# Fillers that shift the transposed activations against multiples of 256 bytes in SBUF, with the weight buffers left where they are

## The chip, the cores and the metric

The kernel runs on one NeuronCore of a Trainium2 chip. The metric is the device time of one execution in microseconds. Three runs of the kernel before took 1163.83, 1164.23 and 1167.16 us; the median is 1164.23 us.

## The reference, cut to what matters

Two transformer blocks run one after the other on 256 tokens of width 1024 in float32. The products that carry most of the arithmetic are these:

```
# first block, layer 0 (attention) and layer 1 (pooling), each followed by a gated feed-forward of width 2816
k, v, q = hx @ w_qkv ...            # with modulation of x by c @ w_mod
x = layer_norm(ALPHA * x + g1 * y)
x = layer_norm(ALPHA * x + g2 * (silu(h @ w_in_g) * (h @ w_in_u)) @ w_out)
# second block
u = rms_norm(x) @ w_in              # sixteen 512-wide slices and one of width 16 (g_lr)
y = sigmoid(gate_a) * y_a + sigmoid(gate_b) * y_b
x = x + y @ w_out
x = x + square(relu(rms_norm(x) @ w_up)) @ w_down      # width 4096
x = x + sigmoid(rms_norm(x) @ w_ple_gate) * (p @ w_ple)
```

Every product has 256 rows of tokens, so every weight is used for two groups of 128 tokens (called t = 0 and t = 1 in the code).

## The kernel before, in words

**Weights.** All weights come in blocks of 128 partitions x 1024 float32 (4096 bytes per partition) in one planned order. `Stream.dma` brings a block into one of eight `raw` buffers. `Stream.split` turns it into two float32r tiles: `hi` (ScalarE copy, L287) and `lo` = raw - hi (VectorE subtraction, L293), eight buffers each. The 80 blocks of modulation weights are reduced on VectorE instead (L271).

**Products.** The operand that TensorE keeps in its array (the stationary operand) is a piece of 128 tokens x 128 features of the transposed activations; the weights stream past it (the moving operand), 512 columns at a time. Each float32 product is made of three float32r matmuls: activation-high x weight-high, activation-high x weight-low, activation-low x weight-high. `mmN` (L378 to L380) does this for a product that is summed over eight pieces into one `mm` tile; `mmK` (L392, L394) and `mmK_tail` (L405 to L407) do it for one row block of weights into the two halves of a `big` tile. Each matmul has a weight load (LDWEIGHTS, shown as PEld) of its own. In the profile `mm<-hi,xTh` is a matmul with moving operand `hi` and stationary operand `xTh`. A few products are done in plain float32, with one instruction in the code and two matmuls in the trace; `keep` (L218) is a filler of that kind, on the tile `crow`.

**Transposed activations.** `xTh` and `xTl` hold the high and low part of the 256 transposed tokens (8 pieces of 256 columns, 8192 bytes per partition each). They are filled by `tr_half`: four transposes on TensorE into a `tr` tile, then a ScalarE copy (L427 or L739) and a VectorE subtraction (L428 or L741). In the feed-forward parts the hidden values are transposed by `tr` (L984) and `trm` (L1608) into `hh0`, `hl0` (t = 0) and `hh1`, `hl1` (t = 1), two buffers each, filled by L427 and L428. Other stationary tiles are `hch`, `hcl` (shown as `xa`, `s`) in the first projections and `obT`, `qkd` in two products of the second block.

**Order.** The order of the instructions on each engine is the order of the program text; `Stream.pump` puts the splitting of further blocks behind each use of a block.

**Where tiles lie.** A tile's address within a partition follows from the pools: pools are stacked in the order in which they are opened, the tiles of a pool follow one another in the order in which their tags first appear, and each starts at a multiple of 32 bytes. In the compiled kernel before, `xTh` starts at byte 18432, `xTl` at 26624, `cst` (identity matrix and tables) at 34816, `crow` at 36160, the eight `raw` at 43008, the eight `hi` at 75776, the eight `lo` at 108544, `xa` at 141312 and `s` at 149504. In the last feed-forward `hh0` starts at 175616, `hl0` at 179712, `hh1` at 183808, `hl1` at 187904 and the output tile `sg` at 192000. The filler tile `pad` ahead of `raw` and the wide `half` tile ahead of `xTh` hold nothing that is used (of `half`, 8 columns are). Of the tiles named, all but `crow` start at a multiple of 256 bytes; `crow` and the `gtmp` tiles of the second block start 64 bytes past one. The low-rank gate product `g_lr` (L1425) uses pieces of 16 columns (64 bytes) of a weight block as the stationary operand, which lie 0, 64, 128 and 192 bytes past multiples of 256 in turn.

Of the kernel before, what the change touches and what calls it, by code (L numbers as in the profile page):

```python
# [10 lines left out]
F32R = mybir.dt.float32r  # L11
# [7 lines left out]
P = 128  # L19
# [154 lines left out]
def body(ctx: ExitStack, tc: tile.TileContext, wst, prm, cst, cst2, poolp, xT_d, cT_d, x_d, head, lam_d,  # L174
# [23 lines left out]
    cp = Pool("cp")  # L198
    ctx.callback(cp.close)
    rg = Pool("rg")  # L200
# [7 lines left out]
    def mmt():  # L208
        return pp.t([P, 512], "mm")

    def trt():
        return pp.t([P, 512], "tr")
# [10 lines left out]
    prm_s = cp.t([P, PRM_W], "prm")  # L223
    mc = [cp.t([P, 48], f"mc{l}") for l in range(2)]
    half_e = cp.t([P, 184], "half")[:, :8]
    xTh = cp.t([P, KD, T], "xTh", F32R)
    xTl = cp.t([P, KD, T], "xTl", F32R)
    cst_s = cp.t([P, CST_W], "cst")
    crow = cp.t([P, D], "crow")
    raw0 = rg.t([P, 368], "pad")  # L230
    G.memset(half_e, -0.5)

    def prmc(n):
# [6 lines left out]
    def is32(key):  # L240
        return key[0] in F32B or (key[0] == "WO" and key[1] // 4 in WOF) or (
            key[0] == "G" and key[2] == 0 and key[1] in GF)
# [116 lines left out]
    def mmN(ps, lh, keys, width=512, off=0, cols=None, mid={}):  # L359
        per = BW // width  # L360
        cols = cols or width
        n = len(keys)
        for i, key in enumerate(keys):
            w32 = st.get32(key) if is32(key) else None
            hi, lo = st.get(key) if w32 is None else (None, None)
            for j in range(per):
                k = i * per + j
                if k in mid:
                    mid[k]()
                if w32 is not None:  # L370
                    TE.matmul(ps, lh(k), w32[:, j * width + off:j * width + off + cols], start=k == 0,
                              stop=i == n - 1 and j == per - 1)
                    continue
                sl = slice(j * width + off, j * width + off + cols)
                h, l = lh(k)
                s = k == 0
                e = i == n - 1 and j == per - 1
                TE.matmul(ps, h, hi[:, sl], start=s, stop=False)  # L378
                TE.matmul(ps, h, lo[:, sl], start=False, stop=False)  # L379
                TE.matmul(ps, l, hi[:, sl], start=False, stop=e)  # L380
# [15 lines left out]
    def mmK_tail(halves, lhs, keys, first=False):  # L396
        for f in range(2):
            sl = slice(f * 512, (f + 1) * 512)
            for i, (lh, key) in enumerate(zip(lhs, keys)):
                if is32(key):  # L400
                    TE.matmul(halves[f], lh, st.get32(key)[:, sl], start=first and i == 0, stop=i == len(keys) - 1)
                    continue
                h, l = lh
                hi, lo = st.get(key)
                TE.matmul(halves[f], h, hi[:, sl], start=first and i == 0, stop=False)  # L405
                TE.matmul(halves[f], h, lo[:, sl], start=False, stop=False)  # L406
                TE.matmul(halves[f], l, hi[:, sl], start=False, stop=i == len(keys) - 1)  # L407

    def halves(ps):
        return [ps[:, 0:512], ps[:, 512:1024]]  # L410

    def xlh(t):
        return lambda k: (xTh[:, k, t * P:(t + 1) * P], xTl[:, k, t * P:(t + 1) * P])

    def mkey(k, n):
        return [k + (i,) for i in range(n)]
# [8 lines left out]
    def split_evac(ps, dh, dl, scale=None):  # L425
        if scale is None:
            A.activation(dh, ps, AF.Copy)  # L427
            V.tensor_tensor(dl, ps, dh.bitcast(F32), op=OP.subtract)  # L428
        else:
            A.activation(dh, ps, AF.Copy, scale=scale)  # L430
            V.scalar_tensor_tensor(dl, ps, scale, dh.bitcast(F32), op0=OP.mult, op1=OP.subtract)
# [372 lines left out]
    for i in range(n_it + 5):  # L804
# [25 lines left out]
        if 3 <= i <= n_it + 2:  # L830
            t, h = items[i - 3]
# [3 lines left out]
        if i >= 5 and items[i - 5][1] % 4 == 3:  # L835
            t, f = items[i - 5][0], items[i - 5][1] // 4
# [108 lines left out]
    def ffn(l, fp, x1_ready, after0, mid1, after1, mid):  # L945
        J = len(FFN_CHUNKS)
        ops_ = None
        hT = {}
        hs = {}

        def gu(j, t, which, ps, mid={}):
            c0, w = FFN_CHUNKS[j]
            n = D * w // (P * BW)
            lh = xlh(t)
            if is32((which, l, j)):
                lh = lambda k: xf[t, k // 4][:, k % 4]
            mmN(ps[:, :w], lh, mkey((which, l, j), n), width=w, mid=mid)

        def do_g(j, t):
            ps = mmt()  # L960
            gu(j, t, "G", ps)
            w = FFN_CHUNKS[j][1]
            h = fp.t([P, 512], f"h{t}", bufs=2)
            A.activation(h[:, :w], ps[:, :w], AF.Silu)  # L964
            hs[j, t] = h

        def do_u(j, t, mid={}):
            ps = mmt()
            gu(j, t, "U", ps, mid)
            w = FFN_CHUNKS[j][1]  # L970
            h = hs[j, t]
            V.tensor_tensor(h[:, :w], h[:, :w], ps[:, :w], op=OP.mult)  # L972

        def fin(j, which):
            c0, w = FFN_CHUNKS[j]
            st.done(*mkey((which, l, j), D * w // (P * BW)))

        def tr(j, t):
            w = FFN_CHUNKS[j][1]
            n = w // P  # L980
            h = hs.pop((j, t))
            ps = trt()
            for i in range(n):
                TE.transpose(ps[:, i * P:(i + 1) * P], h[:, i * P:(i + 1) * P], ident)  # L984
            hh = fp.t([P, 4, P], f"hh{t}", F32R, bufs=2)
            hl = fp.t([P, 4, P], f"hl{t}", F32R, bufs=2)
            pv = ps.rearrange("p (k t) -> p k t", t=P)[:, :n]
            split_evac(pv, hh[:, :n], hl[:, :n])
            hT[j, t] = (hh, hl)

        def o(j, t, done):
            n = FFN_CHUNKS[j][1] // P
            hh, hl = hT.pop((j, t))
            if j == J - 1:
                keys = [("O", l, j, i) for i in range(n)]
                mmK_tail(halves(ops_[t]), [(hh[:, i], hl[:, i]) for i in range(n)], keys)
                if done:
                    st.done(*keys[:HN[l]])
                    st.hold = True
                    st.done(*keys[HN[l]:])  # L1000
                return
            for i in range(n):
                mmK(halves(ops_[t]), (hh[:, i], hl[:, i]), ("O", l, j, i), j == 0 and i == 0, False)
                if done:
                    st.done(("O", l, j, i))

        for j in range(J):
            if j == 0:
                do_g(0, 0)
                do_u(0, 0, {XR[l]: x1_ready})  # L1010
                if XR[l] == 8:
                    x1_ready()
                do_g(0, 1)
                fin(0, "G")
                do_u(0, 1)
                fin(0, "U")
                ops_ = [big(), big()]
            else:
                do_g(j, 0)
                if j == 1:  # L1020
                    tr(0, 1)
                do_g(j, 1)
                fin(j, "G")
                do_u(j, 0)
                do_u(j, 1)
                fin(j, "U")
            if j in mid:
                mid[j]()
            if j < J - 1:
                if j > 0:  # L1030
                    o(j - 1, 0, False)
                tr(j, 0)
                if j > 0:
                    o(j - 1, 1, True)
                    tr(j, 1)
            else:
                tr(j, 0)
                o(j - 1, 0, False)
                tr(j, 1)
                o(j, 0, False)  # L1040
                if l == 0:
                    for b in range(2):
                        st.prescale(("PW", b))
                after0(ops_[0])
                if l == 0:
                    st.hold = True
                o(j - 1, 1, True)
                mid1()
                o(j, 1, True)
                after1(ops_[1])  # L1050
                if l == 1:
                    st.hold = False
                    st.pump()

    fp = Pool("fp")
# [474 lines left out]
    for i, (c, t) in enumerate(seq):  # L1530
        f = int(c[2])
# [55 lines left out]
    fp = Pool("fp3")  # L1587
# [16 lines left out]
    def trm(j, t):  # L1604
        h = hs.pop((j, t))
        ps = trt()
        for i in range(4):
            TE.transpose(ps[:, i * P:(i + 1) * P], h[:, i * P:(i + 1) * P], ident)  # L1608
        hh = fp.t([P, 4, P], f"hh{t}", F32R, bufs=2)
        hl = fp.t([P, 4, P], f"hl{t}", F32R, bufs=2)  # L1610
        split_evac(ps.rearrange("p (k t) -> p k t", t=P), hh, hl)
        hT[j, t] = (hh, hl)

# [161 lines left out]
```

## Time and profile before

| | |
|---|---|
| median of three runs | 1164.23 us |
| profiled execution: its own time | 1166.95 us |
| its span, first to last instruction | 1165.2 us |
| TensorE matmul busy | 1120.5 us, 96% |
| TensorE weight load busy | 884.0 us, 76% |
| VectorE, ScalarE busy | 761.2 us (65%), 560.0 us (48%) |
| mean granted TensorE clock | 0.991 |

A group row of the profile gives line, engine, operation, tile names, shape and count, then busy time and mean duration of one, then idle time before them and what ended it. The duration of a matmul reaches from its first read to a modelled end; successive matmuls overlap, so the distance from start to start is what one matmul costs in a chain. Such distances are read from the timeline.

### The profile page before, as it was taken

To read this page: it belongs to the slowest core of one execution; us is meant where nothing else is said; L and a number is where in the kernel's file an instruction comes from. 1 tells how busy PE (TensorE), PEld (TensorE's weight loads), DVE (VectorE), ACT (ScalarE), POOL (GpSimd) and SP (SyncE) were. 2 spreads that over 40 slices of the span, in tenths; PEclk is the share of its full clock that TensorE was granted. 3 is DMA by queue.
4 is the path that set the end of the run, shared out by engine and by line. 5 is a ranking of instruction groups with operands and counts; after the bars stand their busy time and mean duration, and the time that the engine had idled before them with its cause. 6 is when DMAs were issued, how large, how long until landed. Compare 5 with 4: busy or idle time off the path is not lost. (4 is left out here: it accounts for less than half of the span.)

```text
span 1165.2 us, 14166 instructions
## 1 busy us (share of the span) xinstructions
PE 1120.5 (96%) x5186; PEld 884.0 (76%) x5186; DVE 761.2 (65%) x1114; ACT 560.0 (48%) x913; POOL 22.7 (2%) x35
## 2 busy tenths in 40 slices
PE   7989988899999999999999999999999999999998
PEld 4578665578888876888887687877778877888887
DVE  7988858668886675577446765454545875455555
ACT  3552456454344426534444755457235464444453
POOL 0000000000000000000000110000000000000000
PEclk9999899999999999999999999998999999999999
DMA  9887813669897806568463755452444645454520
GB/s 348 310 275 253 288 57 136 214 224 344 300 392 261 294 20 215 196 225 298 169 226 128 234 194 184 146 167 91 145 145 137 215 154 187 176 201 164 212 93 37
DMA packets 65922, 234.62 MB, mean 201 GB/s; under 512 B 7323, under 2 KB 8347, under 8 KB 65852
## 3 DMA queue, kind: packets, MB, share of 16 engines
q1 hardware_dynamic: 63936, 227.84, 55.2%
q10 hardware_dynamic: 1916, 5.87, 1.5%
q8 instruction: 41, 0.67, 0.2%
q14 instruction: 29, 0.24, 0.1%
HBM read 232.63 MB, written 1.05 MB: 201 GB/s over the span
## 5 line engine op out<-in xcount | busy, mean ns | idle before, releaser
L293 DVE TENSOR_TENSOR lo<-raw,hi 128x1024 fp32r<-128x1024 f32 x316 | 374.6, 1220 | 126.2 <-ACT hi L287 121.8
L287 ACT ACTIVATE hi<-raw 128x1024 fp32r<-128x1024 f32 x316 | 323.1, 1057 | 106.6 <-PE mm L380 56.8
L378 PE MATMUL mm<-hi,xTh 128*128 128x512 f32 (+1 forms) x872 | 339.7, 390 | 7.3 <-ACT xTh L427 4.0
L380 PE MATMUL mm<-hi,xTl 128*128 128x512 f32 (+1 forms) x872 | 334.0, 383 | 2.0 <-DVE xTl L428 1.6
L379 PE MATMUL mm<-lo,xTh 128*128 128x512 f32 (+1 forms) x872 | 333.4, 382 | 1.9 <-DVE lo L293 1.9
L378 PEld LDWEIGHTS mm<-hi,xTh 128*128 128x128 f32 x872 | 165.4, 190 | 45.0 <-ACT xTh L427 5.9
L380 PEld LDWEIGHTS mm<-hi,xTl 128*128 128x128 f32 x872 | 165.1, 189 | 36.1 <-DVE xTl L428 3.3
L379 PEld LDWEIGHTS mm<-lo,xTh 128*128 128x128 f32 x872 | 165.6, 190 | 33.5 <-DVE lo L293 3.4
L271 DVE SCALAR_TENSOR_TENSOR raw<-raw,crow 128x1024 f32<-128x1024 f32 x80 | 96.6, 1218 | 0.0
L392 PE MATMUL big<-hi,hh 128*128 128x512 f32 x256 | 80.6, 396 | 0.0
L392 PE MATMUL big<-lo,hh 128*128 128x512 f32 x256 | 79.2, 391 | 0.0
L394 PE MATMUL big<-hi,hl 128*128 128x512 f32 x256 | 79.0, 390 | 0.0
L427 ACT ACTIVATE hh<-tr 128x512 fp32r<-128x512 f32 (+1 forms) x40 | 23.0, 575 | 84.8 <-PE tr L1608 42.6
L428 DVE TENSOR_TENSOR hl<-tr,hh 128x512 fp32r<-128x512 f32 (+1 forms) x40 | 26.3, 660 | 48.8 <-ACT hh L427 48.0
L394 PEld LDWEIGHTS big<-hi,hl 128*128 128x128 f32 x256 | 48.1, 188 | 10.4
L392 PEld LDWEIGHTS big<-lo,hh 128*128 128x128 f32 x256 | 48.0, 188 | 10.3
L964 ACT ACTIVATE h<-mm 128x512 f32<-128x512 f32 (+1 forms) x24 | 13.4, 563 | 84.1 <-PE mm L380 83.9
L392 PEld LDWEIGHTS big<-hi,hh 128*128 128x128 f32 x256 | 46.7, 188 | 8.6
L422 POOL TENSOR_TENSOR st<-st,half 128x4 f32<-128x4 f32 (+1 forms) x28 | 21.8, 778 | 1045.1 <-DVE st L420 1032.0
L1601 DVE TENSOR_TENSOR h<-h 128x512 f32<-128x512 f32 x16 | 11.0, 688 | 33.6 <-ACT h L1600 33.5
L1600 ACT ACTIVATE h<-mm 128x512 f32<-128x512 f32 x16 | 9.6, 599 | 38.0 <-PE mm L380 38.0
L972 DVE TENSOR_TENSOR h<-h,mm 128x512 f32<-128x512 f32 (+1 forms) x24 | 15.3, 640 | 18.7 <-PE mm L380 18.6
(316 smaller groups left out, 1254.1 us busy)
## 6 DMA issues: line engine op xcount, KB each, us to landing
raw<-in_dram SPq DMA_DIRECT2D x426, 512.0 KB, 5.1
row<-in_dram ACTq DMA_DIRECT2D x8, 512.0 KB, 7.3
tok<-in_dram SPq DMA_DIRECT2D x8, 256.0 KB, 6.9
xa<-in_dram SPq DMA_DIRECT2D x2, 512.0 KB, 5.1
out_dram<-sg SPq DMA_DIRECT2D x3, 256.0 KB, 2.0
pmat<-in_dram ACTq DMA_DIRECT2D x1, 544.0 KB, 12.4
crow<-in_dram ACTq DMA_DIRECT2D x1, 512.0 KB, 4.8
out_dram<-sg SPq DMA_DIRECT2D x2, 128.0 KB, 1.7
```

What stands on the lines that cost most here:

```text
L271: V.scalar_tensor_tensor(raw, raw, 1.0, crow, op0=OP.mult, op1=OP.mult, accum_out=mc[l][:, nb:nb + 1])
L287: A.activation(hi, raw, AF.Copy)
L293: V.tensor_tensor(lo, raw, hi.bitcast(F32), op=OP.subtract)
L378: TE.matmul(ps, h, hi[:, sl], start=s, stop=False)
L379: TE.matmul(ps, h, lo[:, sl], start=False, stop=False)
L380: TE.matmul(ps, l, hi[:, sl], start=False, stop=e)
L392: TE.matmul(halves[f], h, w[:, f * 512:(f + 1) * 512], start=first and b == 0, stop=False)
L394: TE.matmul(halves[f], l, hi[:, f * 512:(f + 1) * 512], start=False, stop=last)
L422: G.tensor_tensor(r, v, half_e[:, :w], op=OP.pow)
L427: A.activation(dh, ps, AF.Copy)
L428: V.tensor_tensor(dl, ps, dh.bitcast(F32), op=OP.subtract)
L972: V.tensor_tensor(h[:, :w], h[:, :w], ps[:, :w], op=OP.mult)
```

## The change

Two filler tiles of 64 bytes are put ahead of `xTh` and between `xTh` and `xTl`, and the filler ahead of the weight buffers is made 128 bytes shorter. The `hh` tiles get 32 and the `hl` tiles 64 unused bytes at their end, so that each later buffer of the pool moves on by as much. The access patterns, the instructions and their order stay.

```diff
     half_e = cp.t([P, 184], "half")[:, :8]
+    pad1 = cp.t([P, 16], "pad1")
     xTh = cp.t([P, KD, T], "xTh", F32R)
+    pad2 = cp.t([P, 16], "pad2")
     xTl = cp.t([P, KD, T], "xTl", F32R)
     cst_s = cp.t([P, CST_W], "cst")
     crow = cp.t([P, D], "crow")
-    raw0 = rg.t([P, 368], "pad")
+    raw0 = rg.t([P, 336], "pad")
...
# in tr (feed-forward of the first block) and in trm (second block)
-            hh = fp.t([P, 4, P], f"hh{t}", F32R, bufs=2)
-            hl = fp.t([P, 4, P], f"hl{t}", F32R, bufs=2)
+            hh = fp.t([P, 4 * P + 8], f"hh{t}", F32R, bufs=2)[:, :4 * P].rearrange("p (k t) -> p k t", t=P)
+            hl = fp.t([P, 4 * P + 16], f"hl{t}", F32R, bufs=2)[:, :4 * P].rearrange("p (k t) -> p k t", t=P)
```

## Rows read from the trace of the kernel before

**Rows 1.** The page: span, busy time of the engines, granted clock in 40 slices.
```profile
span 1165.2 us, 14166 instructions
...
PE 1120.5 (96%) x5186; PEld 884.0 (76%) x5186; DVE 761.2 (65%) x1114; ACT 560.0 (48%) x913; POOL 22.7 (2%) x35
...
PEclk9999899999999999999999999998999999999999
```

**Rows 2.** Groups by line: matmuls and weight loads on the transposed activations.
```profile
L378 PE MATMUL mm<-hi,xTh 128*128 128x512 f32 (+1 forms) x872 | 339.7, 390 | 7.3 <-ACT xTh L427 4.0 <-ACT aT L686 1.5 <-ACT mv L1378 1.2
L380 PE MATMUL mm<-hi,xTl 128*128 128x512 f32 (+1 forms) x872 | 334.0, 383 | 2.0 <-DVE xTl L428 1.6 <-DVE xTl L741 0.4
L379 PE MATMUL mm<-lo,xTh 128*128 128x512 f32 (+1 forms) x872 | 333.4, 382 | 1.9 <-DVE lo L293 1.9
...
L379 PEld LDWEIGHTS mm<-lo,xTh 128*128 128x128 f32 x872 | 165.6, 190 | 33.5 <-DVE lo L293 3.4 <-issue 0.2
...
L392 PE MATMUL big<-hi,hh 128*128 128x512 f32 x256 | 80.6, 396 | 0.0
...
L394 PE MATMUL big<-hi,hl 128*128 128x512 f32 x256 | 79.0, 390 | 0.0
...
L405 PE MATMUL big<-hi,hh 128*128 128x512 f32 x48 | 19.1, 398 | 0.0
...
L392 PE MATMUL big<-hi,xTh 128*128 128x512 f32 x48 | 16.2, 420 | 3.6 <-ACT tok L616 3.6
```

**Rows 3.** Timeline (start, duration, engine, line): matmuls and a load in mid-chain.
```profile
900.42 0.39 PE L378 MATMUL mm<-hi,xTh 128*128 128x512 f32 x1
900.42 0.19 PEld L379 LDWEIGHTS mm<-lo,xTh 128*128 128x128 f32 x1
...
903.82 0.39 PE L378 MATMUL mm<-hi,xTh 128*128 128x512 f32 x1
```

**Rows 4.** Timeline: the first matmuls behind a group of transposes, last feed-forward.
```profile
1005.44 0.63 PE L392 MATMUL big<-lo,hh 128*128 128x512 f32 x2
1005.91 0.62 PE L394 MATMUL big<-hi,hl 128*128 128x512 f32 x2
1006.37 0.62 PE L392 MATMUL big<-hi,hh 128*128 128x512 f32 x2
```

**Rows 5.** Timeline of L1425: stationary pieces of 16 columns, third and last row block.
```profile
781.30 0.28 PE L1425 MATMUL mm<-xTh,hi 128*16 128x256 f32 x1
...
783.23 0.28 PE L1425 MATMUL mm<-xTl,hi 128*16 128x256 f32 x1
```

**Rows 6.** Timeline: feed-forward matmuls of 256 columns, stationary pieces of 128 columns.
```profile
323.27 0.28 PE L378 MATMUL mm<-hi,xTh 128*128 128x256 f32 x1
...
324.59 0.28 PE L380 MATMUL mm<-hi,xTl 128*128 128x256 f32 x1
```

**Rows 7.** Timeline and group row of the filler matmuls on crow.
```profile
426.96 2.31 PE L218 MATMUL tr<-crow 128*128 128x512 f32 x5
...
L218 PE MATMUL tr<-crow 128*128 128x512 f32 x10 | 4.5, 592 | 0.0
```

**Rows 8.** Groups by line: VectorE and ScalarE on tiles at different addresses.
```profile
L427 ACT ACTIVATE hh<-tr 128x512 fp32r<-128x512 f32 (+1 forms) x40 | 23.0, 575 | 84.8 <-PE tr L1608 42.6 <-PE tr L984 42.1
...
L428 DVE TENSOR_TENSOR hl<-tr,hh 128x512 fp32r<-128x512 f32 (+1 forms) x40 | 26.3, 660 | 48.8 <-ACT hh L427 48.0
...
L525 DVE SCALAR_TENSOR_TENSOR junkb<-raw,ropeb 128x1024 bf16<-128x1024 f32 x16 | 19.4, 1219 | 0.0
L525 DVE SCALAR_TENSOR_TENSOR junkb<-raw,crow 128x1024 bf16<-128x1024 f32 x16 | 19.0, 1220 | 1.2 <-DMA raw<-in_dram 1.1
...
L1600 ACT ACTIVATE h<-mm 128x512 f32<-128x512 f32 x16 | 9.6, 599 | 38.0 <-PE mm L380 38.0
...
L1552 ACT ACTIVATE gtmp<-mm 128x512 f32<-128x512 f32 x4 | 2.4, 600 | 9.1 <-PE mm L380 9.0
```

**Rows 9.** DMA issues: the last stores of the result, with KB and time to landing.
```profile
out_dram<-sg SPq DMA_DIRECT2D x2, 128.0 KB, 1.7
```

More of the change, by code (lines that the diff above doesn't have):

```diff
@@ L1608, in trm @@
             TE.transpose(ps[:, i * P:(i + 1) * P], h[:, i * P:(i + 1) * P], ident)
-        hh = fp.t([P, 4, P], f"hh{t}", F32R, bufs=2)
-        hl = fp.t([P, 4, P], f"hl{t}", F32R, bufs=2)
+        hh = fp.t([P, 4 * P + 8], f"hh{t}", F32R, bufs=2)[:, :4 * P].rearrange("p (k t) -> p k t", t=P)
+        hl = fp.t([P, 4 * P + 16], f"hl{t}", F32R, bufs=2)[:, :4 * P].rearrange("p (k t) -> p k t", t=P)
         split_evac(ps.rearrange("p (k t) -> p k t", t=P), hh, hl)
```

## The prediction

> **What bounds the kernel now.** I read the page first. TensorE is busy for 96% of the span, at a granted clock of nine tenths or more, the level of 2.4 GHz, in all but two of 40 slices; the other engines have a third or more of the span to spare [rows 1]. So the span is in the main the number of matmuls times the distance between their starts, and an address can move the time in two ways: through that distance, or through the engines and transfers that feed the chain. The group rows tell which matmuls are concerned. Three groups of 872 use `xTh` or `xTl` as the stationary operand, and the groups of 256 and of 48 on `hh` and `hl` come three times each, as do those of 48 on `xTh` and `xTl`; almost none of them has idle time ahead of it [rows 2]. The timeline then gives the distance. From 900.42 to 903.82 us there are fifteen steps, 226.7 ns each [rows 3]. The load for the next matmul starts with the matmul before and takes 0.19 us, so it is over some 0.04 us before its own matmul starts.
>
> **What moves.** Adding up the tiles of the pools: `xTh` goes from byte 18432 to 18496 (64 past a multiple of 256), `xTl` from 26624 to 26752 (128 past), `cst` from 34816 to 34944 (128), `crow` from 36160 to 36288 (192 instead of 64). The rest of that pool moves by 128 bytes too, and the shorter filler gives these back, so `raw`, `hi`, `lo`, `xa` and `s` stay. In the feed-forwards the buffers of `hh0` come to lie 0 and 32 past, of `hl0` 64 and 128, of `hh1` 192 and 224, of `hl1` 0 and 64; `sg` moves by 384 bytes. Nothing is added to or taken from any queue, no wait is added, and each engine has the instructions it had, in the same order.
>
> **The cost per matmul.** The stationary operand moves for 3 x 872 + 3 x 48 = 2760 matmuls on `xTh` and `xTl` [rows 2] (18 each on `mm` and `tr` tiles are left out). Of 3 x 304 = 912 on `hh` and `hl`, two thirds use `hh`, of whose four buffers one stays at 0, and a third uses `hl`, of whose four buffers one stays: 684 move. Together 3444. One nanosecond more on each would be 3.4 us, 0.3% of the time, about what a measurement of this kernel can tell from no change. So the question is a single nanosecond in 226.7.
>
> The trace of before shows no 128-column float32r load from an address off a multiple of 256. Two rows come near. First, `g_lr` loads pieces of 16 float32r columns that lie 0, 64, 128 and 192 bytes past in turn. From 781.30 to 783.23 us there are seventeen steps through six row blocks, so through all four places, at 0.11 or 0.12 us each and 113.5 ns in the mean [rows 5]. If the place mattered by 10 ns, the steps of three row blocks in four would show it. Second, `keep` has both operands in `crow`, 64 past, with a full load of 128 columns, though in plain float32: five matmuls in 2.31 us of which the last takes 592 ns, so (2310 - 592) / 4 = 429.5 ns a step for two passes of 512 columns, 214.7 ns a pass [rows 7]. That is shorter than the aligned float32r step, so streaming from 64 bytes past costs nothing there; but a slot of 429 ns would hide a load that had grown by many nanoseconds.
>
> Bounds, from both sides. From below: the float32r step could fall to the pass of rows 7, 226.7 - 214.7 = 12.0 ns less, which is -41 us on 3444. From above: a load that takes longer or comes late. With 256 columns streamed, a stationary piece of 128 columns takes 120.0 ns a step (eleven steps from 323.27 to 324.59) [rows 6] against 113.5 ns for a piece of 16 columns [rows 5]; so 6.5 ns hang on how much is loaded, +22 us if a shifted load costs as much again. I take zero: the nearest row in kind is that of L1425, float32r loads at three of the new places, and it shows nothing; and the 0.04 us between the load's end and its matmul [rows 3] would cover a load that grows by less. If that cover is gone, as behind transposes, where the steps are (1005.91 - 1005.44) / 2 = 235 ns [rows 4], a longer load shows there first.
>
> The Trainium skill, page "SBUF — State Buffer", section "Specifications (TRN2)", says that SBUF has lines of 16 bytes and that each step to a new line costs something. All the new offsets are multiples of 32, so a piece of 512 bytes touches 32 lines before and after, and by that rule the upper bound is zero and the sum stays as it is. No run here shows a 16-byte line, so I let it count for little.
>
> **The other engines.** What they write to or read from moved tiles: 40 copies of 575 ns and 40 subtractions of 660 ns on `hh`, `hl` [rows 8], and the like for `xTh`, `xTl`. For an address 64 past the trace has direct pairs: VectorE takes 1220 ns with `crow` (64 past) as an operand and 1219 ns with `ropeb` (0 past), and ScalarE takes 600 ns into `gtmp` (64 past) and 599 ns into `h` (0 past) [rows 8]. I take zero. At 1 ns each way it would be 0.1 us over all 80, and what hides even that is the chain of TensorE, which works on the chunk before while a chunk is evacuated. For 32 and 224 past there is no such row; the bound is a doubled copy and subtraction on the 20 or so of the 40 pairs that go into the second buffers, 20 x (0.575 + 0.660) = 25 us of ScalarE and VectorE time, nearly all behind TensorE, so I take 0 to 2 us for it and put 0 in the sum.
>
> **The transfers.** `sg` is the source of the stores at the end, and the last two land in 1.7 us [rows 9]; `cst` is the target of the first load. A change of a tenth in these two would be 0.3 us. I take zero.
>
> **The sum.** 0 us on the matmuls, 0 on the other engines, 0 on the transfers. The profiled execution took 1166.95 us (a span of 1165.2 and 1.75 around it), 2.7 above the median of the runs shown. With a change of zero the forecast is that median: 1164.2 us.
>
> **The rivals.**
>
> *A, slower: a load that straddles costs more.* The place is every weight load on a shifted tile. If a load is fetched in 256-byte pieces, 512 bytes from a multiple are two pieces and from 64 past are three, while the 64-byte pieces of `g_lr` lie within one at all four places; so rows 5 can't exclude it, and rows 5 and 6 even fit it (6.5 ns for the second piece). Price: 6.5 x 3444 = 22 us, 1187 us. It decides from 1 ns per matmul. Against it: 0.04 us of cover in mid-chain [rows 3]. For it: the step is 12 ns longer than a pass of rows 7 and depends on what is loaded, so the load isn't wholly covered. If it works only behind transposes, on some ten matmuls after each of about 80 groups of transposes (an estimate: 40 that fill `hh` and `hl` [rows 8], and as many others), it is 800 x 6.5 ns = 5 us, 1169 us.
>
> *B, faster: the two streams of TensorE stop colliding.* Before, load and stream start at multiples of 256 together; if the 12 ns are that, shifting takes them away: -41 us, 1123 us. Against it: in rows 5 the load is shifted in three of four row blocks with the stream at 0, and no step is shorter. In part, only where the steps are 235 ns instead of 227 [rows 3, 4], it would be some 800 x 8 ns = 6 us, 1158 us.
>
> The Trainium skill, page "TensorE: Matmul & The Clock Gate", section "Back-to-back issue gap", gives N/2.4 + 2.5 ns for a warm matmul, 215.8 ns for 512 columns as an estimate, against 226.7 here. By that rule 11 ns of each step are not the stream's own, and if the places of the operands were their cause the time would be that of B. The float32 pass of rows 7 agrees with the rule; the trace doesn't say what the rest is.
>
> *C: the change doesn't do what it says.* If a pool rounded sizes up further, the buffers would lie elsewhere, or the weights would move. The arithmetic above gives 43008 for `raw` before and after, so I give it little; its time would be that of no change.
>
> **How the numbers follow.** No effect: 0.54. A in full or in part: 0.31. B in full or in part: 0.11. C and anything else on the feeding engines: 0.04. Of "no effect" I put 0.46 within 0.3% (3.5 us) and 0.04 on each side, for the runs themselves spread over 3.3 us. Of A, 0.02 lies within 0.3%, the rest above; of B, 0.01 within; of C, 0.02 within and 0.02 above. So faster 0.04 + 0.10 = 0.14, the same 0.46 + 0.02 + 0.01 + 0.02 = 0.51, slower 0.04 + 0.29 + 0.02 = 0.35. The range runs from 1158 (B in part) to 1190 (A in full, and a little): it leaves out the full B and an A beyond its price, some 0.15 to 0.2 together. The range of "no effect" alone is 1161 to 1168.
>
> **What would show it right or wrong.** Right: mid-chain steps of 227 ns on `xTh`, `xTl` and all eight `hh` and `hl` buffers alike, and the same counts and durations on the other engines. A: steps above 227 ns on `xTh` and `xTl` (64 and 128 past) but not on `xa`, `s`, `obT` or the buffers at 0. B: steps toward 215 ns on the shifted tiles alone. The forecast is wrong if the mean step of the three `xTh` and `xTl` groups moves by 1 ns or more, or if the span moves by over 3.5 us with TensorE's steps unmoved.

## The result, and the profile of the changed kernel

The changed kernel takes 1173.53 us (median of four runs, 1171.76 to 1177.13); the kernel before took 1164.03 us beside it (four runs, 1163.02 to 1167.16). The ratio is 1.0079 with a 95% interval of 1.0052 to 1.0106: 9.2 us slower, 6.1 to 12.3. (The ratio is worked out from all the runs and isn't the quotient of the two medians; the same holds below.) The forecast of no change was wrong, though the time lies within the range of 1158 to 1190 us.

The profiled execution took 1171.76 us. Its page answers to [rows 1]:

```profile
span 1169.7 us, 14166 instructions
...
PE 1127.9 (96%) x5186; PEld 882.1 (75%) x5186; DVE 761.4 (65%) x1114; ACT 559.3 (48%) x913; POOL 22.7 (2%) x35
...
PEclk9999999999999999999999999999999999999999
```

The counts are those of before, and so is the work of VectorE and ScalarE. TensorE alone is busy for longer, by 7.4 us, though its granted clock is nine tenths or more in every slice, where before had two slices of eight. The two spans differ by only 4.5 us because the profiled execution of before was 2.9 us above its median and this one is 1.8 us below.

The group rows, against [rows 2], hardly tell:

```profile
L380 PE MATMUL mm<-hi,xTh 128*128 128x512 f32 (+1 forms) x872 | 343.7, 394 | 6.9 <-ACT xTh L429 4.0 <-ACT aT L688 1.5 <-ACT mv L1380 1.1
...
L382 PE MATMUL mm<-hi,xTl 128*128 128x512 f32 (+1 forms) x872 | 334.3, 383 | 2.0 <-DVE xTl L430 1.6 <-DVE xTl L743 0.4
...
L381 PEld LDWEIGHTS mm<-lo,xTh 128*128 128x128 f32 x872 | 164.4, 189 | 33.7 <-DVE lo L295 2.7 <-issue 0.2
```

The mean duration of a matmul went from 390 to 394 ns on the first row and stayed at 383 on the second, and the load that is shown as 190 ns before is shown as 189 now. Such durations end at a modelled point. What a matmul costs is the distance between starts, and there the change is plain. The timeline (start, duration, engine, line) in the place of [rows 3]:

```profile
904.86 0.40 PE L380 MATMUL mm<-hi,xTh 128*128 128x512 f32 x1
904.86 0.19 PEld L381 LDWEIGHTS mm<-lo,xTh 128*128 128x128 f32 x1
...
908.32 0.40 PE L380 MATMUL mm<-hi,xTh 128*128 128x512 f32 x1
```

These are again fifteen steps, and they take 3.46 us instead of 3.40: 230.7 ns each, not 226.7. On `hh` and `hl` in the last feed-forward:

```profile
1007.96 0.63 PE L394 MATMUL big<-lo,hh 128*128 128x512 f32 x2
1008.43 0.63 PE L396 MATMUL big<-hi,hl 128*128 128x512 f32 x2
...
1012.62 0.63 PE L396 MATMUL big<-hi,hl 128*128 128x512 f32 x2
```

The first pair behind the transposes takes 0.47 us as before [rows 4]. But before the steps fall to 227 ns after some ten of them, and here they don't: from 1007.96 to 1012.62 there are twenty, 233 ns each. The same chunk in the kernel before, ten steps of 226 to 227 ns:

```profile
1007.75 0.62 PE L392 MATMUL big<-hi,hh 128*128 128x512 f32 x2
...
1010.01 0.62 PE L394 MATMUL big<-hi,hl 128*128 128x512 f32 x2
```

From all start-to-start distances of the two traces, for steps between two float32r matmuls of 512 columns at the full clock that wait for nothing and are shorter than 260 ns: 3113 of 227.6 ns before, 3129 of 230.9 ns after. The 3.3 ns more, times 3129, are 10.2 us, which covers the 9.2 us. Of these the steps within `xTh` and `xTl` (some 2030) carry 7.1 us. They are unequal, sorted by the tile whose matmul ends the step:

| step to a matmul on | before | after |
|---|---|---|
| `xTh` (second, from `xTh`) | 227.7 ns | 235.4 ns |
| `xTl` (from `xTh`) | 227.3 ns | 228.6 ns |
| `xTh` (first, from `xTl`) | 227.7 ns | 229.5 ns |
| `xa`, `s`, `obT`, which didn't move | 226.8, 227.5, 228.1 ns | 226.9, 227.5, 228.1 ns |

### The profile page after: what moved, and what is told of

Same layout as the page of the kernel before. It is cut to its first block, busy times and chain, and to the rows that moved or that the text cites. A ratio compares the mean times of both kernels' runs of the same rounds, so it can differ in the third digit from the quotient of the medians.

```text
span 1169.7 us, 14166 instructions
## 1 busy us (share of the span) xinstructions
PE 1127.9 (96%) x5186; PEld 882.1 (75%) x5186; DVE 761.4 (65%) x1114; ACT 559.3 (48%) x913; POOL 22.7 (2%) x35
## 5 line engine op out<-in xcount | busy, mean ns | idle before, releaser
L380 PE MATMUL mm<-hi,xTh 128*128 128x512 f32 (+1 forms) x872 | 343.7, 394 | 6.9 <-ACT xTh L429 4.0
```

## The experiments

"Place" below is where a tile starts past a multiple of 256 bytes. "Distance" is the place of the stationary piece that is loaded, less the place of the weights that stream while it is. In the kernel before every float32r load of 128 columns has place 0 and distance 0; in the changed one the weights are still at place 0, so the two numbers are the same. The theories, by the letters that the expectations use:

- **L**: the load's own place decides, as a load that straddles 256-byte pieces (rival A of the prediction).
- **L2**: the difference between the places of two loads in a row decides (64 and 128 in turn).
- **H**: the `hh` and `hl` tiles carry the loss. **O**: other engines, on the shifted tiles, carry it.
- **R**: the distance between load and stream, modulo 256 bytes, decides.

Where a kernel has one run only, what it shows rests on its steps and not on its time, since single runs of the kernel before spread from 1158.7 to 1169.8 us. Steps given as means are taken from starts, as above, and are those with 512 columns streamed unless the text says otherwise. Three means in brackets follow the first three rows of the table above.

**One part at a time.** Only the fillers at `xTh`, `xTl`:

```diff
+    pad1 = cp.t([P, 16], "pad1")
     xTh = cp.t([P, KD, T], "xTh", F32R)
+    pad2 = cp.t([P, 16], "pad2")
     xTl = cp.t([P, KD, T], "xTl", F32R)
...
-    raw0 = rg.t([P, 368], "pad")
+    raw0 = rg.t([P, 336], "pad")
```

> Only the fillers around xTh and xTl (64 and 128 bytes past a multiple of 256); hh and hl as before. Theory L (a weight load from a shifted address makes its own step longer): the mid-chain steps on xTh and xTl are those of the changed kernel (about 235, 229 and 230 ns in the three kinds, 231 in the mean, against 227), those on hh and hl are 227 again; 2760 x 3.6 ns = 10 us, so 7 to 12 us slower than before, most of the whole change. Theory O (the other engines, cst, crow or the stores are what costs): steps on xTh stay at 231 or fall to 227, and the time is anywhere, but the steps don't account for it. Theory H (the hh and hl buffers are what costs): within 3 us of before.

1171.05 against 1163.16 us: 1.0055, interval 1.0035 to 1.0075, so 6.4 us (4.1 to 8.7).

```profile
904.82 0.40 PE L380 MATMUL mm<-hi,xTh 128*128 128x512 f32 x1
...
908.29 0.40 PE L380 MATMUL mm<-hi,xTh 128*128 128x512 f32 x1
```

Fifteen steps of 231.3 ns, with the same three unequal ones (235.3, 228.7, 229.5); `hh` and `hl` are back at 227 to 228. Then the other part alone, which leaves the pool of `xTh` untouched:

```diff
-            hh = fp.t([P, 4, P], f"hh{t}", F32R, bufs=2)
-            hl = fp.t([P, 4, P], f"hl{t}", F32R, bufs=2)
+            hh = fp.t([P, 4 * P + 8], f"hh{t}", F32R, bufs=2)[:, :4 * P].rearrange("p (k t) -> p k t", t=P)
+            hl = fp.t([P, 4 * P + 16], f"hl{t}", F32R, bufs=2)[:, :4 * P].rearrange("p (k t) -> p k t", t=P)
```

> Only the longer hh and hl tiles (0, 32, 64, 128, 192, 224 bytes past); xTh and xTl as before. Theory L: steps on hh and hl of 230 to 233 ns in the mean, on xTh and xTl 227 as before; 912 x 3.5 ns = 3 us slower, at the edge of what can be measured. Theory H: 7 to 12 us slower. Theory O: no change of steps.

1167.15 us: 1.0028, interval 1.0009 to 1.0048, so 3.3 us (1.0 to 5.6).

```profile
904.06 0.39 PE L378 MATMUL mm<-hi,xTh 128*128 128x512 f32 x1
...
907.46 0.39 PE L378 MATMUL mm<-hi,xTh 128*128 128x512 f32 x1
```

`xTh` and `xTl` are at 226.7 ns again and only steps on `hh` and `hl` are at 230 to 232. Each part slows its own tiles and no others, and 6.4 + 3.3 = 9.7 us is the whole. H falls: that part carries a third.

**The same fillers, 256 bytes long.** As many tiles move, by as much or more, but every place stays 0:

```diff
+    pad1 = cp.t([P, 64], "pad1")
...
+    pad2 = cp.t([P, 64], "pad2")
...
-    raw0 = rg.t([P, 368], "pad")
+    raw0 = rg.t([P, 240], "pad")
...
# hh and hl: 4 * P + 64
```

> Control: the same fillers, but each of 256 bytes, so that all tiles move and all still start at multiples of 256. Theory L and any theory of the place within 256 bytes: all steps 227 ns, time within 3 us of before. If moving the tiles costs in itself (other banks further up, other distances to the weights): slower by 5 to 12 us as the changed kernel.

1166.93 us: 1.001, interval 0.9988 to 1.0032, and steps of 227 ns throughout, fifteen of them in these rows:

```profile
904.47 0.39 PE L380 MATMUL mm<-hi,xTh 128*128 128x512 f32 x1
...
907.87 0.39 PE L380 MATMUL mm<-hi,xTh 128*128 128x512 f32 x1
```

It isn't that the tiles move, or that other tiles move with them, but where they lie within 256 bytes.

**Both activation tiles at one place.** `xTh` and `xTl` both 64 past (`pad1` of 16 columns, no `pad2`, `raw0` [P, 352]); the loads that follow one another no longer differ in place.

> xTh and xTl both 64 bytes past, hh and hl as before. Theory L, each load by its own place: the steps whose next load is from xTl now grow from 229 to what a load 64 past costs, so the mean over the three kinds rises from 231 to 232 or more. Rival L2 (it is the difference of places between a load and the load before it that costs): now that all loads have the same place, steps fall back to 227. Rival R (it is the place of the load relative to the streamed weights, all at 0, that costs): as L here.

1176.28 us in one run.

```profile
904.93 0.39 PE L379 MATMUL mm<-hi,xTh 128*128 128x512 f32 x1
...
908.43 0.39 PE L379 MATMUL mm<-hi,xTh 128*128 128x512 f32 x1
```

Fifteen steps of 233.3 ns; the three are now alike (233.5, 233.4, 233.1). L2 falls, for without a difference the loss is larger. And 233.3 - 226.7 = 6.6 ns is as large as the price that rival A had from rows 5 and 6 (6.5 ns); what that is worth is said in the next section.

**Both at 128, and both at 32.** `pad1` of 32 and of 8 columns, `raw0` shortened by as much.

> xTh and xTl both 128 bytes past a multiple of 256, hh and hl as before. If a load is fetched in pieces of 128 bytes (512 bytes are four pieces from 128 past, five from 64 past): all steps 227 ns and the time of before within 3 us. If in pieces of 256 (two against three): steps of 233 ns as with both 64 past, about 12 us slower. If the cost grows by halves with the place: steps of 229 to 230 ns, about 6 us slower.

1172.92 against 1166.66 us: 1.0064, interval 1.0041 to 1.0087.

> xTh and xTl both 32 bytes past. Pieces of 128 or of 256 bytes: steps of 233 ns as with both 64 past. A cost that grows by halves with the place: 236 to 240 ns. Pieces of 32 bytes or less would have given no cost at 64 either.

1173.90 us in one run. The first two rows are of the kernel with 128, the last two of that with 32:

```profile
968.18 0.39 PE L379 MATMUL mm<-hi,xTh 128*128 128x512 f32 x1
...
971.66 0.40 PE L379 MATMUL mm<-hi,xTh 128*128 128x512 f32 x1
```

```profile
904.85 0.40 PE L379 MATMUL mm<-hi,xTh 128*128 128x512 f32 x1
...
908.35 0.40 PE L379 MATMUL mm<-hi,xTh 128*128 128x512 f32 x1
```

Steps of 232.0 and 233.3 ns: 32, 64 and 128 cost about the same. So far L and R both fit.

**Does the stream's place count?** First the weights move with the activations: all of `xTh`, `xTl`, `raw`, `hi` and `lo` lie 64 past (`cst` and `crow` between them move by 64 bytes too), and what follows them keeps its place (192 bytes are added behind the last `lo`).

```diff
+    pad1 = cp.t([P, 16], "pad1")
     xTh = cp.t([P, KD, T], "xTh", F32R)
...
             lo = rg.t([P, BW], "lo", F32R, bufs=R)
+            if self.nw == 0:
+                rg.t([P, 48], "pad3")
```

> xTh, xTl and all weight buffers (raw, hi, lo) 64 bytes past, everything else at multiples of 256 as before. Theory L (the load's own place): steps on xTh and xTl of 233 ns as with the weights at 0. Rival R (load and stream must start at different places within 256 bytes to collide): steps of 227 ns, since both are shifted alike.

1168.3 us in one run.

```profile
904.71 0.39 PE L381 MATMUL mm<-hi,xTh 128*128 128x512 f32 x1
...
908.11 0.39 PE L381 MATMUL mm<-hi,xTh 128*128 128x512 f32 x1
```

226.7 ns: loads of `xTh` and `xTl` at place 64 are as cheap as at 0 once the stream is at 64 too. It is `hh`, `hl`, `xa`, `s` and `obT`, at place 0 and now at distance -64, that rose, to 228.7 to 229.6 ns in the mean. Then the weights alone, 64 past (`raw0` [P, 384] and the same `pad3`; every activation at place 0):

> Only the weight buffers 64 bytes past; all transposed activations at multiples of 256. Theory L: steps of 227 ns on xTh, xTl, hh and hl. Rival R: 233 ns. If a shifted stream costs on its own account: more than 227 on all, xa and s as well.

1169.98 us in one run.

```profile
905.22 0.39 PE L380 MATMUL mm<-hi,xTh 128*128 128x512 f32 x1
...
908.65 0.39 PE L380 MATMUL mm<-hi,xTh 128*128 128x512 f32 x1
```

228.7 ns, with all activations unmoved: the three steps are (230.4, 227.8, 229.3), and `hh` is at 229 to 231. L would have these at 227; it falls here. R gets the direction right but not the size, for it was expected at 233: a distance of -64 costs about 2 ns and one of 64 costs 6.6. That a shifted stream costs by itself would fit these rows too, `xa` and `obT` included (229.6 and 229.5), but not those of the experiment just above, where the stream is at 64 and `xTh` and `xTl` are at 226.7. R stands.

**All distances in one kernel.** In the feed-forwards, 256 spare bytes per `hh` and `hl` tile let each chunk of hidden values start at a place of its own, `hh` and `hl` alike, 0, 32, ..., 224 in turn; the rest is the kernel before.

```diff
+            oh, ol = HO[(j + 4 * t) % 8], LO_[(j + 4 * t) % 8]
-            hh = fp.t([P, 4, P], f"hh{t}", F32R, bufs=2)
+            hh = fp.t([P, 4 * P + 64], f"hh{t}", F32R, bufs=2)[:, oh:oh + 4 * P].rearrange("p (k t) -> p k t", t=P)
# hl the same with ol
```

> Only hh and hl are shifted, both of a chunk alike, by 0, 32, 64, ... 224 bytes, one place per chunk and token group in turn; everything else as before (weights at 0). Rival R (it is the distance between load and stream within 256 bytes that costs): at 0 steps of 227 ns, at 32, 64 and 128 of 232 to 234 as for xTh and xTl, at 192 of 229 as with the weights alone 64 past (the same distance), between these at the rest. Theory L (straddling): 233 at all but 0, 192 and 224 too.

Then the same with the places 16, 48, ..., 240:

> As the scan of 32, but 16, 48, 80, ... 240 bytes past. Rival R: a smooth course between the values of the scan of 32, none below 227. If 16 bytes matter as such (a line of 16 or 32 bytes shared with the stream): 16 and 240 near 227 or well off the neighbours. If a place better than 0 exists, a step below 226 ns shows it.

And the first again, with the weights, `xTh` and `xTl` moved to 128 past (`pad1` [P, 32], `pad3` [P, 32]):

> The scan of 32 with xTh, xTl and all weights 128 bytes past. Rival R: the course of the scan moves by 128: 227 ns at 128, 232 to 233 at 0, 160 and 192, 229 at 64; xTh and xTl at 227. Theory L: lowest at 0. A mixture (place of the load and distance) would leave neither 0 nor 128 at 227.

They took 1166.72, 1165.18 and 1169.43 us. The timelines of the first (place 0, then place 128, each 22 steps from row to row) and of the third (the same):

```profile
974.30 0.62 PE L394 MATMUL big<-hi,hh 128*128 128x512 f32 x2
...
979.29 0.39 PE L396 MATMUL big<-hi,hl 128*128 128x512 f32 x1
...
1066.01 0.64 PE L394 MATMUL big<-hi,hh 128*128 128x512 f32 x2
...
1071.13 0.40 PE L396 MATMUL big<-hi,hl 128*128 128x512 f32 x1
```

```profile
977.36 0.64 PE L397 MATMUL big<-hi,hh 128*128 128x512 f32 x2
...
982.48 0.40 PE L399 MATMUL big<-hi,hl 128*128 128x512 f32 x1
...
1069.10 0.61 PE L397 MATMUL big<-hi,hh 128*128 128x512 f32 x2
...
1074.09 0.39 PE L399 MATMUL big<-hi,hl 128*128 128x512 f32 x1
```

With the weights at 0 place 0 takes 226.8 ns and place 128 takes 232.7; with the weights at 128 it is the other way round. The mean step in ns by place, without the first ten steps of a chunk (27 to 78 steps each); behind transposes those are unsteady at any place, 224 to 236 ns in the kernel before:

| place | 0 | 32 | 64 | 96 | 128 | 160 | 192 | 224 |
|---|---|---|---|---|---|---|---|---|
| weights at 0 | 226.7 | 233.4 | 233.3 | 234.4 | 233.1 | 233.4 | 228.8 | 233.2 |
| weights at 128 | 232.7 | 233.6 | 228.9 | 233.1 | 226.7 | 233.4 | 233.2 | 234.2 |

The lower row is the upper one moved by 128 bytes: by distance, both have 227 at 0, 229 at 192 (that is, -64), and 233 to 234 elsewhere. In the third kernel `xTh` and `xTl`, at 128 with the weights, are at 227.6 ns as before, and `xa`, `s` and `obT`, now at distance -128, are at 232 to 233. This is what R says and no other theory does. At the odd multiples of 16 the steps are 233 at 48 and 112, 232 to 233 at 80, 144 and 208, 230 at 176, and 227.6 at 240. So the smooth course that was expected of R failed: 240 lies near 227 beside a 224 at 233. At 16 there are two courses: every chunk with t = 0 has steps of 226.7 ns from end to end, every chunk with t = 1 has 233.3; at 144 one chunk takes 226.6 and the other five 233. The four quick chunks are just those that start straight behind matmuls on `xTl` that were already at 227; the eight slow ones start behind transposes or behind a chunk at place 176. So at these two places the step seems to keep the course in which the chain arrives; no run varied that alone. No chunk in any of the three has a settled mean below 226.6, so with 512 columns the distance of the kernel before is as good as any that was found.

**Two loads at different distances.** As above, with `hh` and `hl` of a chunk at different places:

> hh and hl of a chunk at different places: (64,128), (128,64), (64,0), (0,64), (128,0), (0,128), (192,0), (32,128) in turn; weights at 0. If each load adds its own cost (6.7 ns at 64 and 32, 5.8 at 128, 2.4 at 192, of three loads two are hh): mean steps of 233, 233, 231, 229, 231, 229, 228, 233. If loads of different places relieve each other, as the 231.1 of xTh 64 and xTl 128 suggests: (64,128) 231, and no more than that for the pairs with a 0.

1165.58 us. Mean steps in `mmK` by (place of `hh`, place of `hl`), again without the first ten: (64, 128) 231.0, (128, 64) 233.4, (64, 0) 232.1, (0, 64) 230.1, (128, 0) 233.2, (0, 128) 233.3, (192, 0) 229.3, (32, 128) 231.7 ns. Chunks of the first and the fifth of these pairs, again 22 steps each:

```profile
973.11 0.63 PE L394 MATMUL big<-hi,hh 128*128 128x512 f32 x2
...
978.20 0.62 PE L396 MATMUL big<-hi,hl 128*128 128x512 f32 x2
...
1064.86 0.64 PE L394 MATMUL big<-hi,hh 128*128 128x512 f32 x2
...
1070.00 0.62 PE L396 MATMUL big<-hi,hl 128*128 128x512 f32 x2
```

They take 231.4 and 233.6 ns. Two thirds of the loads are on `hh`. If each load paid by its own distance (0 at 0, 6.6 at 64, 6.5 at 128), (0, 128) would be 228.9 and (64, 0) 231.1; they are 233.3 and 232.1. So one load at a distance slows its neighbours too, and some mixtures, (64, 128) above all, cost less than either place alone. The order of the loads counts as well: `mmK` has four on `hh` and then two on `hl`, `mmK_tail` has two and one, and there (128, 64) takes 229.7 ns and (0, 128) 231.3. The sum over single loads fails. The rival hits (64, 128), but the pairs with a 0 were to take no more than 231 and three of them take 232 to 233; what rule there is instead stayed open.

**Everything 64 past.** What was still missing is a test of L and R in whole times. One filler of 64 bytes and nothing taken back, so that all that follows `xTh`, weights and `hh` included, lies 64 past: all distances 0, nearly all loads straddling.

```diff
+    pad1 = cp.t([P, 16], "pad1")
     xTh = cp.t([P, KD, T], "xTh", F32R)
```

> One filler of 64 bytes ahead of xTh and none taken away, so that xTh, xTl, all weight buffers and every tile behind them lie 64 bytes past multiples of 256, the transposed activations and the weights alike. Rival R (only the distance between load and stream within 256 bytes costs): all steps 227 ns, and the time of before within 3 us (0.3%). Theory L (the load's own place costs): all steps 233 ns and 20 us slower, to 1184 us. If anything else of the shift costs (stores, evacuations, identity matrix), slower with steps of 227.

1166.53 against 1163.95 us: 1.0018, interval 0.9997 to 1.0039.

```profile
905.04 0.39 PE L379 MATMUL mm<-hi,xTh 128*128 128x512 f32 x1
...
908.44 0.39 PE L379 MATMUL mm<-hi,xTh 128*128 128x512 f32 x1
```

226.7 ns, and no loss that can be told from none. At 6.5 ns for each straddling load the time would have been above 1184 us.

## Why the prediction was wrong

*What bounds the kernel*: right. The span is the number of matmuls times the distance of their starts, and the 10.2 us that those distances grew by cover the 9.2 us of the result.

*The step that failed* is the one that chose between the bounds: "I take zero: the nearest row in kind is that of L1425, float32r loads at three of the new places, and it shows nothing". What the runs showed in its place is that a full load at a distance from a stream of 512 columns costs 2 to 8 ns of a step of 227 (1 to 8 in the mixture of the changed kernel), 10.2 us in all. The row of L1425 has loads of 16 columns under a stream of 256; the loads in question have 128 columns under a stream of 512. The row shared the type and the places, but neither length, and both turn out to count. Nor is that row itself free of the places. With both tiles at 64 its loads are at the same distances modulo 256 bytes as before, in another order, and yet the eighteen steps between these rows take 120.0 ns each and not 113.5:

```profile
787.50 0.28 PE L1426 MATMUL mm<-xTh,lo 128*16 128x256 f32 x1
...
789.66 0.28 PE L1426 MATMUL mm<-xTh,lo 128*16 128x256 f32 x1
```

And full loads under a stream of 256 columns (240 of the 2760 matmuls on `xTh` and `xTl`) go the other way. The row of [rows 6] in the same kernel, twelve steps:

```profile
326.42 0.28 PE L379 MATMUL mm<-hi,xTh 128*128 128x256 f32 x1
...
327.78 0.28 PE L379 MATMUL mm<-hi,xTh 128*128 128x256 f32 x1
```

These are 113.3 ns each against 120.0 in [rows 6]. In the mean over all such steps, 119.8 ns at distance 0, wherever the pair lies, became 113.4 at 64, and about 118 at 32, 128 and -64. With this shorter stream the same place is the dearest that was tried.

*The bound from above*, 6.5 ns that "hang on how much is loaded", was a misreading of rows 5 and 6: with both tiles at 64 the full load has the step of 113.3 ns and the load of 16 columns that of 120.0. So the 6.5 ns between the two rows can't be put down to the length of the load, and the 0.31 that was given to rival A rested on that in part.

*The cover of 0.04 us* failed too. It was read from the end of the load's row [rows 3]. In the kernel with both tiles at 64 that same row is still 0.19 us long, and the mean of its group, 190 ns in [rows 2], is 188, while the step grew by 6.6 ns:

```profile
L380 PEld LDWEIGHTS mm<-lo,xTh 128*128 128x128 f32 x872 | 164.3, 188 | 36.2 <-DVE lo L294 2.4 <-issue 0.2
```

The recorded length of a load doesn't contain what it loses, so no cover can be worked out from it.

*Rival A* had the place (steps on the shifted tiles, not on `xa`, `s`, `obT`) and the price, 6.5 ns against 6.6 measured with both tiles at 64, but the wrong cause: a load straddles just as much in the last experiment, and costs nothing there. That the price agreed was luck as far as these runs show, since the rows it came from don't say what was read from them. Its time of 1187 us missed as well, because the changed kernel puts `xTh` at 64 and `xTl` at 128, and this mixture costs 235.4 + 228.6 + 229.5 - 3 x 227.6 = 10.7 ns in three steps and not 19.5. Times about 900 threes of `xTh`, `xTl` that is some 10 us as an upper estimate; 7.1 us is the sum over the steps that wait for nothing, and 6.4 us the time of that part alone.

*Rival B* had the right pair, load and stream, and for streams of 512 columns the wrong sign. There, starting at the same place modulo 256 bytes isn't the collision but the one case in which every chunk was free, and no distance gave a settled mean step below 226.6 ns. For streams of 256 columns its sign was right: 119.8 ns became 118.3 in the changed kernel, which is under 0.4 us over 240 matmuls. The 12 ns between that and the pass of [rows 7] have another cause, which nothing here shows.

The Trainium skill, page "TensorE: Matmul & The Clock Gate", section "Step-by-step: what each phase is for", says that TensorE has two independent read ports and that loading the next weights takes no read bandwidth from the running matmul. The runs don't bear out that the two reads are independent: with the same load and the same stream, a step takes 226.7 or 233 ns by the distance of their places alone. The measurement decides. Whether the reads meet in a port, a bank of the memory, or elsewhere isn't shown by any of these runs.

*The other engines and the transfers* were rightly put at zero:

```profile
L429 ACT ACTIVATE hh<-tr 128x512 fp32r<-128x512 f32 (+1 forms) x40 | 23.0, 575 | 88.7 <-PE tr L986 45.2 <-PE tr L1610 43.5
L430 DVE TENSOR_TENSOR hl<-tr,hh 128x512 fp32r<-128x512 f32 (+1 forms) x40 | 26.3, 660 | 51.4 <-ACT hh L429 50.6
L527 DVE SCALAR_TENSOR_TENSOR junkb<-raw,crow 128x1024 bf16<-128x1024 f32 x16 | 19.0, 1219 | 1.3 <-DMA raw<-in_dram 1.2
```

575 and 660 ns as in [rows 8], though these tiles now lie at 0 to 224 past, 1219 ns on `crow` now 192 past, and the last stores still land in 1.7 us, as in [rows 9]. Theory O falls by these rows. *Rival C* falls by the steps.

*The count*: 684 of the 912 on `hh` and `hl` were taken to move. But the chunk whose `hh` stayed at place 0 is paired with `hl` at 64, and its steps rose as well, to 230 to 232 ns; what a step costs hangs on the loads beside it too.

Four things stay open: the mechanism; why costs don't add; the two courses at 16 and 144; and why shorter streams and shorter loads answer differently. One row of the changed kernel belongs to the last of these:

```profile
785.73 0.28 PE L1427 MATMUL mm<-xTh,hi 128*16 128x256 f32 x1
...
788.07 0.28 PE L1427 MATMUL mm<-xTl,hi 128*16 128x256 f32 x1
```

Here `xTh` and `xTl` are the streams. Twenty steps take 2.34 us, 117 ns each against 113.5 before, so loads of 16 columns lose some here too, less than the 6.5 ns with both tiles at 64. With everything at 64 it is 113.5 again, and with both tiles at 128 it is 113.8.

## What to carry to other kernels

Where float32r matmuls of 512 columns follow one another, each with a load of 128 columns of its own, let the stationary and the moving operand start at the same place modulo 256 bytes; a filler ahead of both is harmless, and one ahead of either costs up to 8 ns of 227 per matmul. Don't carry this to other shapes untried: with 256 columns a distance of 64 bytes made the step shorter, 113.4 ns instead of 119.8. Read such a cost from the distances between starts, since the recorded lengths of matmul and load hide it. And when rows of before are to stand for one that isn't there, take the row that is alike in the amount moved, in the load and in the stream, not only in type and address.

## What the runs showed of the hardware that was not expected

- The step of a float32r matmul (512 columns streamed, 128 loaded, full clock) is 226.7 ns when load and stream start at the same place modulo 256 bytes, 232 to 234.5 ns at most other distances, and 228.8 ns at -64. It depends on the difference of the two places and not on either: the course by place moves with the weights.
- With 256 columns streamed and 128 loaded it is the other way: 119.8 ns at the same place, 113.4 ns at a distance of 64, and about 118 ns at 32, 128 and -64.
- At a distance of 16 bytes, chunks of one kernel took either 226.7 or 233.3 ns a step, each from end to end, whatever their place modulo 2048 bytes; the quick ones started straight behind a chain at 227. At -16 the mean was 227.6.
- One shifted load among aligned ones slows the others: with `hh` at 0 (two thirds of the loads) and `hl` at 128, the mean step in `mmK` is 233.3 ns, that of all loads shifted.
- Loads of 16 columns under 256 streamed take 113.5 ns a step with the streams at 0, and 120.0 ns with the streams at 64, at the same distances modulo 256 bytes in another order; so for them the distance alone doesn't decide. With the streams at 64 and 128 in turn it is 117 ns.
